# A gated DeltaNet kernel: inverses from 16-row blocks, and GpSimd's arithmetic on other engines

## The chip, the cores and the metric

The kernel runs on one core of a Trainium2 chip. The metric is the device time of one execution in microseconds, the median of several runs. The engines are PE (TensorE; PEld is its weight load), DVE (VectorE), ACT (ScalarE), POOL (GpSimd) and SP (SyncE, which here issues the DMAs). Each engine works through its own queue in order.

## The reference

A backbone of four layers over 512 tokens (256 of context, 256 noisy) of 1024 features. Layers 0 and 3 are gated DeltaNet (GDN), layer 1 is an S5 scan, layer 2 is RWKV-7; a SwiGLU FFN follows each. Of the GDN layers this matters here:

```python
def gated_delta_chunked(q, k, v, g, beta, s0):          # per head and direction
    gcum = jnp.cumsum(g, axis=-1)
    decay = jnp.where(incl, jnp.exp(jnp.where(incl, diff, 0.0)), 0.0)
    m = jnp.where(strict, jnp.einsum('bhnik,bhnjk->bhnij', k_beta, k) * decay, 0.0)
    t_inv = lax.linalg.triangular_solve(eye + m, ...)   # lower, unit diagonal
    u = jnp.einsum('bhnij,bhnjd->bhnid', t_inv, v_beta)
    w = jnp.einsum('bhnij,bhnjk->bhnik', t_inv, k_beta * jnp.exp(gcum)[..., None])
    def step(S, xs):
        v_new = u_c - jnp.einsum('bhck,bhkd->bhcd', w_c, S)
        o_c = jnp.einsum('bhck,bhkd->bhcd', q_c, S) + jnp.einsum('bhij,bhjd->bhid', a_c, v_new)
        S = S * gt[..., None, None] + jnp.einsum('bhck,bhcd->bhkd', k_c, v_new)
        return S, o_c
```

There are 8 key heads with two value heads each, and two directions. All data are float32.

## The kernel before, in words

The kernel takes chunks of 128 tokens, so a key head has 16 matrices of 128 rows to invert (4 chunks, 2 value heads, 2 directions). `Net.gdn` works head by head. While the recurrences of head g run (`GdnCore.chains`, 48 steps), other work is emitted beside them in lanes: the dense products and convolutions of coming heads (`key`, `query`, `values`, `gate`), the output of the head before (`finish`, `project`), the decay-weighted Gram matrices of head g + 2 (`gram`), the scores of head g + 1 (`scores`), and the inverses of head g + 1 (`invert`, which calls `inv128`). The chains of head g + 1 need those inverses. A scheduler then sets the order of each engine's queue from the emitted program; it may move an instruction a long way.

Three pieces are touched.

**The inverses.** `inv128` first copies the sixteen 32-row diagonal blocks of each matrix to D (`pool_copy`, L409, on POOL). `fsub` transposes them (L428) and solves 31 rows one after another: row i is a product on DVE (L439, into fsP) and a subtraction on DVE (L441, into fsT), each depending on the one before; the operands have 16 to 136 elements per partition. L444 and L471 transpose the result. After that `inv128` joins blocks of 32 to 64 and 64 to 128 rows by small matmuls (`mul`, L463) with copies from PSUM between (`evac`, which alternates ACT, L402, and DVE, L406).

**The weight split.** Every weight tile is loaded raw, rounded to its upper part on ACT (L128) and the lower part is the difference (L129, 128x512). Which engine subtracts is `self.sub`: DVE in general, POOL inside `gdn` (L537). Products use three matmuls (L135 to L137). The same `self.sub` splits activations (L159), and `norm` sets it to POOL and DVE in turn.

**Other arithmetic on POOL in `GdnCore`:** in `gram` the product of decay and Gram matrix (L1220) and its scaling per chunk (L1222, 16 per head); in `scores` the queries' decay (L1280); in `chains` the keys' decay kd (L1335, 12 per head); in `finish` a sum (L1362) and a product (L1369).

Of the kernel before, what the change touches and what calls it, by code (L numbers as in the profile page):

```python
# [19 lines left out]
P = 128  # L20
# [7 lines left out]
class Net:  # L28
# [67 lines left out]
    def banks(self, **n):  # L96
        """PSUM of a phase: banks by use, next to the two of the dense products"""
# [22 lines left out]
    def wtile(self, src):  # L120
        """-> the two parts of each block of 128 columns"""
# [84 lines left out]
    def norm(self, l, which, ts=slice(0, T), f32=None, f3=False):  # L206
# [8 lines left out]
        for k in range(KD):  # L215
# [15 lines left out]
        self.sub = nc.vector  # L231
# [86 lines left out]
    def gdn_ab(self, j, gp):  # L318
        """gates: rows of cumulated log decay (two exact parts) and per-token columns"""
# [43 lines left out]
    def conv_silu(self, ps, cw, out, segs=(0, 1)):  # L363
        """depthwise conv over each segment, then silu as h (1 + tanh h) with h half the value"""
# [19 lines left out]
    def gdn_E(self, gp, RS, ngc, m, tag, bufs, bank, eb=None):  # L384
        """E[p, f] = exp(-|gc_p - gc_f|) of one head and direction, all four chunks"""
# [25 lines left out]
    def fsub_marks(self, gp):  # L411
        """which rows (parity, unit) of a block hold the odd columns, and which the even ones"""
# [34 lines left out]

    def inv128(self, fs, A, par, W):
        """in place of one head's 16 matrices: units 0-7 the transposed inverse of 1 + L; units 8-15 the inverse, its
        rows times the token's factor"""  # L450
# [8 lines left out]
        def bank(w):  # L459
            return self.ps("i").rearrange("p (u c) -> p u c", c=w)  # L460
# [9 lines left out]
        UD = new("fsUD")  # L470
        nc.vector.transpose(UD, TD)  # L471
# [20 lines left out]
        # blocks off the diagonal of the 64-row blocks  # L492
# [34 lines left out]
    def gdn(self, l, j, last):  # L527
        nc, tc, d = self.nc, self.tc, self.d
        with self.banks(c=2, o=1, w=1, i=2), self.weights(3), \
# [5 lines left out]
            with self.open_h():  # L535
                self.norm(l, 0)
                self.sub = nc.gpsimd  # L537
# [4 lines left out]
                lanes = [Lane(core.invert(0), 41, 41),  # L542
# [8 lines left out]
                for g in range(8):  # L551
# [12 lines left out]
                    if g < 7:  # L564
                        lanes += [Lane(core.invert(g + 1), 41, 40), Lane(core.scores(g + 1), 8, 26, 16)]
# [16 lines left out]
    def s5_params(self):  # L582
        """discretisation; rows (direction, state), columns groups. A group's row of 40: powers of the diagonal by
        position (real, imaginary), input factor, diagonal, rotations exp(8 i theta 2 ** x)"""
# [8 lines left out]
        with tc.tile_pool(name="s5p", bufs=1, reuse_waits="tile") as sp:  # L593
# [37 lines left out]
            # powers of the diagonal  # L631
# [13 lines left out]
            # input factor (a - 1) / lambda  # L645
# [32 lines left out]
    def s5_prep(self, sp, pool):  # L678
        """what the mixer takes of its parameters, four groups at a time"""
# [14 lines left out]
        for i in range(16):  # L694
# [38 lines left out]
            # rotations exp(8 i theta m), m = 0 .. 63  # L733
# [18 lines left out]
            # lag kernels -7 .. 7, the skip at lag 0  # L752
# [14 lines left out]
            # block Toeplitz rows (7 - t, channel): windows of the lags  # L767
# [985 lines left out]
```

## Time and profile before

| | |
|---|---|
| runs | 4284.14 us median of 3 (4276.6 to 4288.32) |
| profiled execution | span 4284.9 us, 0.8 us above that median; it has no other time than its span |
| busy in the span | PE 87%, PEld 67%, DVE 64%, ACT 44%, POOL 32% |
| matmul instructions | 24810 |
| mean granted TensorE clock | 0.888 of full speed |
| layer 0, GDN | about 60 to 928 us of the span |
| layer 3, GDN | about 3350 to 4085 us |

In the rows, times count from the start of the span. Inside each GDN layer three stretches can be told apart: the first inverse, before any chain runs (142 to 221 and 3423 to 3501 us); six heads at their steady pace (309 to 869 and 3573 to 4029 us, each from the first chain product of one head to that of the sixth head after it); and an end without inverses. Layer 3 needs queries, gates and outputs of the second half of the tokens alone, so it has less matmul work per head. A busy engine may still run slowly, and a mean over a whole span mixes stages that have different limits.

### The profile page before, as it was taken

How to read it: one execution, taken by the hardware profiler on the slowest of the kernel's cores; microseconds unless marked ns; L12 is line 12 of the kernel's file. 1: busy time of each engine (PE TensorE's matmuls, PEld its weight loads, DVE VectorE, ACT ScalarE, POOL GpSimd, SP SyncE). 2: the span in 40 equal slices, each digit the busy share in tenths (PEclk: the TensorE clock that was granted, in tenths of full speed). 3: DMA queues.
4: the chain of work that ended last, by engine and by line, in shares of the span. 5: the costliest groups of instructions: out<-in, count | busy, mean ns of one | idle time of the engine just before them, and what ended most of it. 6: DMA issues, size and time to landing. Idle time of an engine off the chain costs nothing. (4 is left out here: it accounts for less than half of the span.)

```text
span 4284.9 us, 67673 instructions
## 1 busy us (share of the span) xinstructions
PE 3730.8 (87%) x24810; PEld 2890.9 (67%) x24810; DVE 2723.6 (64%) x5871; ACT 1865.7 (44%) x3991; POOL 1382.9 (32%) x1623
## 2 busy tenths in 40 slices
PE   4889889879999798999794999998999768888799
PEld 1566667757777686777573766665777556766698
DVE  4788878757786744333954556564333598888665
ACT  4455555553333334222543334334222455556454
POOL 1665566442222200000213434320000465666400
PEclk8889999989999899999895656678999888898899
DMA  4312111126666623443351111002444111111155
GB/s 148 111 59 78 49 45 50 43 73 191 201 203 180 239 86 123 156 157 115 129 168 57 43 31 36 28 11 91 153 158 145 60 35 43 58 52 48 45 174 161
DMA packets 243596, 432.22 MB, mean 101 GB/s; under 512 B 27968, under 2 KB 53184, under 8 KB 240832
## 3 DMA queue, kind: packets, MB, share of 16 engines
q1 hardware_dynamic: 243264, 427.90, 31.3%
q8 instruction: 195, 3.19, 0.3%
q14 instruction: 137, 1.12, 0.1%
HBM read 383.49 MB, written 44.30 MB: 100 GB/s over the span
## 5 line engine op out<-in xcount | busy, mean ns | idle before, releaser
L128 ACT CAST whi<-wraw 128x512 fp32r<-128x512 f32 (+1 forms) x906 | 553.3, 613 | 1143.4 <-PE psd L136 622.1
L129 DVE TENSOR_TENSOR wlo<-wraw,whi 128x512 fp32r<-128x512 f32 (+1 forms) x646 | 447.2, 695 | 647.8 <-ACT whi L128 633.5
L135 PE MATMUL psw<-hhi,whi 128*128 128x512 f32 (+1 forms) x1536 | 597.0, 389 | 22.3 <-ACT sz L1177 11.9
L137 PE MATMUL psw<-hhi,wlo 128*128 128x512 f32 (+1 forms) x1536 | 579.2, 377 | 0.0
L136 PE MATMUL psw<-hlo,whi 128*128 128x512 f32 (+1 forms) x1536 | 579.0, 377 | 0.1
L129 POOL TENSOR_TENSOR wlo<-wraw,whi 128x512 fp32r<-128x512 f32 x260 | 352.1, 1357 | 195.4 <-ACT whi L128 181.4
L135 PEld LDWEIGHTS psw<-hhi,whi 128*128 128x128 f32 x1536 | 304.0, 198 | 93.6 <-ACT sz L1177 13.1
L137 PEld LDWEIGHTS psw<-hhi,wlo 128*128 128x128 f32 x1536 | 300.8, 196 | 53.0 <-issue 2.1
L136 PEld LDWEIGHTS psw<-hlo,whi 128*128 128x128 f32 x1536 | 302.7, 197 | 48.5 <-issue 2.9
L135 PE MATMUL psd<-hhi,whi 128*128 128x512 f32 (+1 forms) x784 | 296.6, 378 | 16.1 <-ACT hhi L158 16.1
L441 DVE TENSOR_TENSOR fsT<-fsT,fsP 128x126 f32<-128x126 f32 (+22 forms) x744 | 287.9, 387 | 13.5
L136 PE MATMUL psd<-hlo,whi 128*128 128x512 f32 (+1 forms) x784 | 291.7, 372 | 3.8 <-DVE hlo L159 3.4
L137 PE MATMUL psd<-hhi,wlo 128*128 128x512 f32 (+1 forms) x784 | 289.9, 370 | 0.4 <-DVE wlo L129 0.4
L439 DVE TENSOR_TENSOR fsP<-fsL,fsT 128x126 f32<-128x126 f32 (+22 forms) x744 | 279.4, 376 | 14.0
L135 PE MATMUL psd<-fh,whi 128*128 128x512 f32 (+1 forms) x704 | 261.3, 371 | 0.0
L136 PE MATMUL psd<-fl,whi 128*128 128x512 f32 (+1 forms) x704 | 257.3, 366 | 0.0
L137 PE MATMUL psd<-fh,wlo 128*128 128x512 f32 (+1 forms) x704 | 256.8, 365 | 0.0
L239 DVE SCALAR_TENSOR_TENSOR X<-psd,modT,X 128x256 f32<-128x256 f32 x376 | 166.1, 477 | 128.1 <-PE psd L137 127.1
L171 PE MATMUL psm<-mraw,cs 128*32 128x256 f32 x1280 | 141.2, 412 | 63.3 <-DMA mraw<-in_modw 62.2
L135 PEld LDWEIGHTS psd<-hhi,whi 128*128 128x128 f32 x784 | 149.9, 191 | 63.4 <-ACT hhi L158 21.6
L136 PEld LDWEIGHTS psd<-hlo,whi 128*128 128x128 f32 x784 | 149.6, 191 | 35.4 <-DVE hlo L159 5.2
L137 PEld LDWEIGHTS psd<-hhi,wlo 128*128 128x128 f32 x784 | 149.7, 191 | 25.5 <-DVE wlo L129 0.8
(509 smaller groups left out, 8493.7 us busy)
## 6 DMA issues: line engine op xcount, KB each, us to landing
mraw<-in_modw SPq DMA_DIRECT2D x384, 256.0 KB, 3.4
wraw<-in_ffnin SPq DMA_DIRECT2D x352, 256.0 KB, 2.9
wraw<-in_gdn_qkvz SPq DMA_DIRECT2D x192, 256.0 KB, 2.7
wraw<-in_ffnout SPq DMA_DIRECT2D x160, 256.0 KB, 2.8
wraw<-in_gdn_out SPq DMA_DIRECT2D x64, 256.0 KB, 2.7
wraw<-in_rwkv_rkv SPq DMA_DIRECT2D x48, 256.0 KB, 3.0
s5ca<-ca SPq DMA_DIRECT2D x32, 256.0 KB, 3.3
s5in<-it SPq DMA_DIRECT2D x32, 256.0 KB, 4.2
```

The source lines that it names most:

```text
L128: nc.scalar.copy(hi[:, :n], raw[:, :n])
L129: self.sub.tensor_tensor(lo[:, :n], raw[:, :n], hi[:, :n].bitcast(F32), op=ALU.subtract)
L135: mm(out, whi, ahi, start=start, stop=False)
L136: mm(out, whi, alo, start=False, stop=False)
L137: mm(out, wlo, ahi, start=False, stop=stop)
L171: nc.tensor.matmul(ps[64 * x + 32 * q:64 * x + 32 * q + 32, :256], self.cs[:, k, :], w[:, q * 256:q * 256 + 256], start=(k == 0), stop=(k ...
L239: nc.vector.scalar_tensor_tensor(self.X[:, f, c], ps[:, c], self.modT[l][:, gate, f, s:s + 1], self.X[:, f, c], op0=ALU.mult, op1=ALU.add)
L439: nc.vector.tensor_tensor(pv, L[:, i + 1:, i:i + 1].to_broadcast([P, n, m]), X[:, i:i + 1, 0:m].to_broadcast([P, n, m]), op=ALU.mult)
L441: nc.vector.tensor_tensor(X[:, i + 1:, 0:m], X[:, i + 1:, 0:m], pv, op=ALU.subtract)
```

## The change

`sub16` takes the place of `fsub` in the GDN layers (the RWKV layer keeps `fsub`). It takes the two 16-row diagonal blocks of each 32-row block, solves both at once in 14 steps of two DVE operations with at most 56 elements, and joins them to 32 rows by two rounds of 64 small matmuls, with DVE transposes and one PSUM read between. `inv128` is then as before, with 29 emitted steps instead of 41. POOL's arithmetic in the GDN layers goes to DVE (weight splits, activation splits, L1220 and L1222 as one fused operation, L1280, L1362, L1369) and to ACT (the copies to D, kd). `norm` no longer alternates.

```diff
 def norm(...):
-                self.sub = (nc.gpsimd, nc.vector)[k % 2]
                 self.split(h[:, ts], self.hhi[k][:, ts], self.hlo[k][:, ts])
+    def sub16(self, fs, mk, D, block, bank, new):
+        even, low, odd, eye, top = mk
+        L = fs.tile([P, 1024], F32, name=self.nm("fsL"), tag="fsL")
+        A, X = [L[:, x:x + 256].rearrange("p (r c) -> p r c", c=16) for x in (512, 768)]
+        L = L[:, :512].rearrange("p (r i) -> p r i", i=32)
+        nc.vector.transpose(L, D.rearrange("p u (h r) -> p r h u", h=2))
+        nc.vector.scalar_tensor_tensor(A, L[:, :, 0:16], even, L[:, :, 16:32], op0=ALU.mult, op1=ALU.add)
+        nc.vector.tensor_tensor(X, eye, A, op=ALU.subtract)
+        for i in range(1, 15):
+            n, m = 15 - i, i
+            pv = pr[:, :n * m].rearrange("p (r c) -> p r c", c=m)
+            nc.vector.tensor_tensor(pv, A[:, i + 1:, i:i + 1].to_broadcast([P, n, m]),
+                                    X[:, i:i + 1, 0:m].to_broadcast([P, n, m]), op=ALU.mult)
+            nc.vector.tensor_tensor(X[:, i + 1:, 0:m], X[:, i + 1:, 0:m], pv, op=ALU.subtract)
+            yield
+        nc.scalar.activation(E[:, :, 0:16], xt, AF.Copy, scale=even)
+        nc.scalar.activation(E[:, :, 16:32], xt, AF.Copy, scale=low)
+        nc.vector.transpose(TD.rearrange("p u (h c) -> p c h u", h=2), E)
+        nc.vector.transpose(UD, TD)
+        pv = bank(16)
+        for u in range(16):
+            for b in range(4):
+                mm(pv[q[b], u], block(q[b], u), TD[q[b], u, 0:16], start=True, stop=True)
+        nc.vector.scalar_tensor_tensor(R, pv, odd, top..., op0=ALU.mult, op1=ALU.add)
+        pv = bank(16)
+        for u in range(16):
+            for b in range(4):
+                mm(pv[q[b], u], UD[q[b], u], R[q[b], u], start=True, stop=True)
+        self.evac(TD[:, :, 0:16], pv)
+        nc.vector.transpose(UD, TD)
 def inv128(...):
-            self.pool_copy(D[x], Z[x, :, x])
+            nc.scalar.copy(D[x], Z[x, :, x])
-        TD = yield from self.fsub(fs, par, D, new)
-        nc.vector.transpose(UD, TD)
+        TD, UD = yield from self.sub16(fs, par, D, lambda x, u: Z[x, u, x], bank, new)
 def gdn(...):
-                self.sub = nc.gpsimd
-                        lanes += [Lane(core.invert(g + 1), 41, 40), ...]
+                        lanes += [Lane(core.invert(g + 1), 29, 40), ...]
 class GdnCore: gram
-            nc.gpsimd.tensor_tensor(e, e, g, op=ALU.mult)
-                nc.gpsimd.tensor_scalar(M[...], e[:, c * P:c * P + P], be[:, hd, c:c + 1], 0.0, ...)
+                nc.vector.scalar_tensor_tensor(M[...], e[:, cs], be[:, hd, c:c + 1], g[:, cs],
+                                               op0=ALU.mult, op1=ALU.mult)
 scores
-            nc.gpsimd.tensor_tensor(eb[:, tq], eb[:, tq], q[:, tq], op=ALU.mult)
+            nc.vector.tensor_tensor(eb[:, tq], eb[:, tq], q[:, tq], op=ALU.mult)
 chains
-                    nc.gpsimd.tensor_scalar(kd, kt[:, cs], ec[hd][:, c:c + 1], 0.0, ...)
+                    nc.scalar.activation(kd, kt[:, cs], AF.Copy, scale=ec[hd][:, c:c + 1])
 finish
-        nc.gpsimd.tensor_tensor(v2(sq), v2(sq), q2, op=ALU.add)
+        nc.vector.tensor_tensor(v2(sq), v2(sq), q2, op=ALU.add)
-        nc.gpsimd.tensor_tensor(z, z, v2(r), op=ALU.mult)
+        nc.vector.tensor_tensor(z, z, v2(r), op=ALU.mult)
```

How the queues change is read from the built programs (the line numbers of the changed kernel are its own). First, GpSimd's queue in layer 3 at the steady pace, about a sixth of one head, before:

```order
L129 TENSOR_TENSOR wlo_31625<-wraw_31623,whi_31624 128x512
L129 TENSOR_TENSOR wlo_31631<-wraw_31629,whi_31630 128x512
L1335 TENSOR_SCALAR kd_31478<-kt_30718,el_30936 128x128
L1220 TENSOR_TENSOR E_31601<-E_31601,acc 128x512
L1335 TENSOR_SCALAR kd_31551<-kt_30718,el_30971 128x128
L129 TENSOR_TENSOR wlo_31723<-wraw_31721,whi_31722 128x512
L1220 TENSOR_TENSOR E_31676<-E_31676,acc 128x512
```

In the changed kernel, all of its queue for one head there (sk, a power of four numbers, and three memsets stood there before as well):

```order
L1270 TENSOR_TENSOR sk_32450<-ss_32447,half_6062_30263 128x4
L543 MEMSET M_31515 32x8x32
L544 MEMSET M_31515 32x8x32
L578 MEMSET M_31515 64x8x64
```

Nothing that reads a whole tile is left on GpSimd in a GDN layer.

Second, VectorE's queue in layer 3 while a head's rows are solved, before (x and S are the chain's two DVE steps, X the residual):

```order
L439 TENSOR_TENSOR fsP_31226<-fsL_31206,fsT_31208 128x120
L1316 SCALAR_TENSOR_TENSOR x_31423<-psc_29471,neg_29664,V_30755 128x128
L239 SCALAR_TENSOR_TENSOR X<-psd_31635,modT_84,X 128x256
L441 TENSOR_TENSOR fsT_31208<-fsT_31208,fsP_31226 128x20x6
L439 TENSOR_TENSOR fsP_31226<-fsL_31206,fsT_31208 128x133
```

and in the changed kernel near the end of the 14 steps (L481 and L483 are the new pair, L1378 is x, L1403 is S):

```order
L129 TENSOR_TENSOR wlo_32425<-wraw_32423,whi_32424 128x512
L481 TENSOR_TENSOR fsP_32256<-fsL_32224 128x26
L1403 SCALAR_TENSOR_TENSOR S_32402<-S_32213,gt_31801,psc_30265 128x128
L380 SCALAR_TENSOR_TENSOR kT_32196<-t_32278,kT_32196 128x512
L1378 SCALAR_TENSOR_TENSOR x_32415<-psc_30266,neg_30478,V_31647 128x128
L374 SCALAR_TENSOR_TENSOR q_32197<-t_32341,cw_30297,q_32197 128x255
L129 TENSOR_TENSOR wlo_32513<-wraw_32511,whi_32512 128x512
L483 TENSOR_TENSOR fsL_32224<-fsL_32224,fsP_32256 128x2x13
```

The weight splits now stand in the queue of the chain's x and S.

Third, TensorE's queue in layer 3, where the first round of the new small matmuls of that head stands (L497, 64 in all):

```order
L497 MATMUL psi_32634<-fsTD_32606,M_31515 32x16 x12
L1398 MATMUL psc_30265<-w_32509,kd_32540 128x128
L135 MATMUL psd_32569<-Y_32201,whi_32518 128x256
L136 MATMUL psd_32569<-Y_32201,whi_32518 128x256
L137 MATMUL psd_32569<-Y_32201,wlo_32519 128x256
L135 MATMUL psd_32569<-Y_32201,whi_32518 128x256
L136 MATMUL psd_32569<-Y_32201,whi_32518 128x256
L137 MATMUL psd_32569<-Y_32201,wlo_32519 128x256
L1376 MATMUL psc_30266<-S_32353,kT_30599 128x128
L497 MATMUL psi_32634<-fsTD_32606,M_31515 32x16 x31
```

The scheduler splits the rounds into pieces among the large products: 74 pieces for the 16 rounds of layer 0, 41 for those of layer 3.

## Rows read from the trace of the kernel before

**Rows 1.** Stretches of layer 0: length, then busy us of each engine.

```profile
core 0: us, PE busy (x) PEld busy (x) DVE busy (x) ACT busy (x) POOL busy (x), PEclk, DMA share, GB/s
142.00:221.00 79.00, 63.43 (x477) 42.38 (x477) 64.13 (x133) 35.98 (x86) 45.70 (x50) 0.85 0.33 107
309.00:869.00 560.00, 497.41 (x3556) 388.16 (x3555) 449.63 (x965) 309.04 (x677) 327.75 (x364) 0.95 0.17 54
869.00:928.00 59.00, 45.69 (x214) 35.62 (x215) 19.42 (x48) 26.89 (x44) 22.39 (x27) 0.86 0.06 18
```

**Rows 2.** The same of layer 3.

```profile
3423.00:3501.00 78.00, 53.69 (x440) 44.35 (x438) 71.00 (x142) 40.32 (x100) 49.51 (x55) 0.81 0.17 55
3573.00:4029.00 456.00, 374.39 (x3241) 318.37 (x3242) 398.82 (x897) 262.06 (x619) 279.66 (x340) 0.91 0.16 52
```

**Rows 3.** Groups by line, 309 to 869 us: count, busy, mean ns, idle before.

```profile
L129 POOL TENSOR_TENSOR wlo<-wraw,whi 128x512 fp32r<-128x512 f32 x91 | 122.7, 1350 | 71.5 <-ACT whi L128 66.8 <-PE psw L137 2.9 <-PE psw L136 1.3
L441 DVE TENSOR_TENSOR fsT<-fsT,fsP 128x126 f32<-128x126 f32 (+22 forms) x177 | 76.1, 430 | 3.4
L439 DVE TENSOR_TENSOR fsP<-fsL,fsT 128x126 f32<-128x126 f32 (+22 forms) x176 | 71.2, 404 | 3.6
L239 DVE SCALAR_TENSOR_TENSOR X<-psd,modT,X 128x256 f32<-128x256 f32 x96 | 41.9, 476 | 27.1 <-PE psd L137 26.6
L376 DVE SCALAR_TENSOR_TENSOR t<-t,cw,t 128x508 f32<-128x508 f32 (+1 forms) x48 | 41.8, 871 | 4.4 <-ACT t L372 3.9
L1316 DVE SCALAR_TENSOR_TENSOR x<-psc,neg,V 128x128 f32<-128x128 f32 x73 | 25.0, 346 | 22.5 <-PE psc L1314 21.9
```

**Rows 4.** Groups by line, 3573 to 4029 us.

```profile
L129 POOL TENSOR_TENSOR wlo<-wraw,whi 128x512 fp32r<-128x512 f32 x88 | 117.7, 1342 | 37.1 <-ACT whi L128 31.9 <-DVE t L376 4.0 <-DVE X L239 0.6
L441 DVE TENSOR_TENSOR fsT<-fsT,fsP 128x126 f32<-128x126 f32 (+22 forms) x176 | 78.7, 447 | 2.5
L439 DVE TENSOR_TENSOR fsP<-fsL,fsT 128x126 f32<-128x126 f32 (+22 forms) x176 | 78.0, 443 | 2.8
```

**Rows 5.** Longest waits of PE, 3573 to 4029 us: total us, times, longest.

```profile
PE psc L1319 <- DVE x L1316: 15.6, 11, 4.3
PE psi L1199 <- DVE kT L382: 13.2, 4, 4.4
```

**Rows 6.** DVE in order of time: start us, us, line.

```profile
3576.10 0.30 DVE L439 TENSOR_TENSOR fsP<-fsL,fsT 128x133 f32<-128x133 f32 x1
...
3578.37 1.25 DVE L441 TENSOR_TENSOR fsT<-fsT,fsP 128x126 f32<-128x126 f32 x1
```

**Rows 7.** POOL at the same time.

```profile
3577.82 0.37 POOL L1335 TENSOR_SCALAR kd<-kt,el 128x128 f32<-128x128 f32 x1 [3.60 <-PE psc L1336]
3578.16 1.31 POOL L129 TENSOR_TENSOR wlo<-wraw,whi 128x512 fp32r<-128x512 f32 x1
```

**Rows 8.** DVE in order of time, operations of three sizes.

```profile
3560.39 0.68 DVE L1203 TENSOR_TENSOR acc<-psi,SU 128x512 f32<-128x512 f32 x1
3560.98 0.21 DVE L441 TENSOR_TENSOR fsT<-fsT,fsP 128x56 f32<-128x56 f32 x1
3561.11 0.42 DVE L382 SCALAR_TENSOR_TENSOR sz<-t,sz 128x256 f32<-128x256 f32 x1
```

**Rows 9.** DVE in order of time, the last row of a block and a transpose.

```profile
196.43 0.17 DVE L439 TENSOR_TENSOR fsP<-fsL,fsT 128x16 f32<-128x16 f32 x1
196.85 1.17 DVE L444 STREAM_TRANSPOSE fsTD<-fsT 128x512 f32<-128x512 f32 x1
```

**Rows 10.** PE in order of time: large products and pieces of small ones.

```profile
267.32 1.20 PE L463 MATMUL psi<-fsTD,M 32*32 32x32 f32 x64 [0.66 <-DVE fsTD L444]
...
538.53 0.38 PE L1331 MATMUL pso<-E,w 128*128 128x128 f32 x2
538.75 0.39 PE L1336 MATMUL psc<-w,kd 128*128 128x128 f32 x2
539.07 0.43 PE L463 MATMUL psi<-fsTD,M 32*32 32x32 f32 x14
```

More of the change, by code (lines that the diff above doesn't have):

```diff
@@ L446, in fsub, with sub16_consts @@
         return TD
+    def sub16_consts(self, gp):
+        nc = self.nc
+        even, low = self.fsub_marks(gp)
+        odd = gp.tile([P, 1], F32, name=self.nm("par"), tag="par2")
+        nc.vector.tensor_scalar(odd, low, -1.0, None, op0=ALU.mult)
+        eye = gp.tile([P, 16, 16], F32, name=self.nm("eye16"), tag="eye16")
+        nc.gpsimd.memset(eye, 0.0)
+        nc.gpsimd.memset(eye.rearrange("p r c -> p (r c)")[:, ::17], 1.0)
+        top = gp.tile([P, 16], F32, name=self.nm("top16"), tag="top16")
+        nc.gpsimd.memset(top, 0.0)
+        for b in range(4):
+            nc.gpsimd.affine_select(out=top, in_=top, compare_op=ALU.not_equal, fill=1.0, base=-32 * b,
+                                    pattern=[[-1, 16]], channel_multiplier=1)
+        return even, low, odd, eye, top
@@ new lines, in sub16 @@
+    def sub16(self, fs, mk, D, block, bank, new):
+        nc = self.nc
+        mm = nc.tensor.matmul
+        even, low, odd, eye, top = mk
+        q = [slice(32 * b, 32 * b + 32) for b in range(4)]
+        L = fs.tile([P, 1024], F32, name=self.nm("fsL"), tag="fsL")
[5 more added lines that the diff above has]
+        yield
+        pr = fs.tile([P, 64], F32, name=self.nm("fsP"), tag="fsP")
+        for i in range(1, 15):
[4 more added lines that the diff above has]
+            nc.vector.tensor_tensor(X[:, i + 1:, 0:m], X[:, i + 1:, 0:m], pv, op=ALU.subtract)
+            yield
+        E = new("fsE")
+        xt = X.rearrange("p r c -> p c r")
+        nc.scalar.activation(E[:, :, 0:16], xt, AF.Copy, scale=even)
+        nc.scalar.activation(E[:, :, 16:32], xt, AF.Copy, scale=low)
+        TD = new("fsTD")
+        nc.vector.transpose(TD.rearrange("p u (h c) -> p c h u", h=2), E)
+        yield
+        UD = new("fsUD")
+        nc.vector.transpose(UD, TD)
[3 more added lines that the diff above has]
+                mm(pv[q[b], u], block(q[b], u), TD[q[b], u, 0:16], start=True, stop=True)
+        yield
+        R = A
+        nc.vector.scalar_tensor_tensor(R, pv, odd, top.unsqueeze(1).to_broadcast([P, 16, 16]), op0=ALU.mult,
+                                       op1=ALU.add)
+        pv = bank(16)
+        for u in range(16):
+            for b in range(4):
+                mm(pv[q[b], u], UD[q[b], u], R[q[b], u], start=True, stop=True)
+        yield
+        self.evac(TD[:, :, 0:16], pv)
+        UD = new("fsUT")
+        nc.vector.transpose(UD, TD)
+        yield
+        return TD, UD
@@ L459, in bank @@
         def bank(w):
-            return self.ps("i").rearrange("p (u c) -> p u c", c=w)
+            return self.ps("i")[:, :min(T, 16 * w)].rearrange("p (u c) -> p u c", c=w)
         def mul(o, x, y):
@@ L541, in gdn @@
                     pass
-                lanes = [Lane(core.invert(0), 41, 41),
+                lanes = [Lane(core.invert(0), 29, 41),
                          Lane(chain(core.query(0), core.values(0), core.key(1)), 22, 30),
@@ L1151, in __init__ @@
         self.bank = [net.ps("c") for _ in range(2)]
-        self.par = net.fsub_marks(gp)
+        self.par = net.sub16_consts(gp)
         self.W = self.new("W", 1, [P, 8, 64])
@@ L1219, in gram @@
             e = net.gdn_E(self.gp, self.RS, self.ngc, m, "Em", 2, "i")
-            nc.gpsimd.tensor_tensor(e, e, g, op=ALU.mult)
             for c in range(4):
-                nc.gpsimd.tensor_scalar(M[:, (hd % 2) * 8 + (hd // 2) * 4 + c], e[:, c * P:c * P + P],
-                                        be[:, hd, c:c + 1], 0.0, op0=ALU.mult, op1=ALU.add)
+                cs = slice(c * P, c * P + P)
+                nc.vector.scalar_tensor_tensor(M[:, (hd % 2) * 8 + (hd // 2) * 4 + c], e[:, cs], be[:, hd, c:c + 1],
+                                               g[:, cs], op0=ALU.mult, op1=ALU.mult)
             yield
```

5 lines of the change are left out of this document (1 added, 4 removed).

## The prediction

> **What bounds the kernel now.** I read first the busy times by stretch, then the groups by line in the steady stretches, then the waits, and last a few moments in order of time.
>
> The change acts in layers 0 and 3 alone, so the shares of the whole span say little. In the six steady heads of layer 0 a head takes 560 / 6 = 93.3 us; PE is busy 89% of that, DVE 80%, POOL 59%, ACT 55% [rows 1]. In layer 3 a head takes 456 / 6 = 76.0 us, with PE at 82% and DVE at 87% [rows 2]. The longest waits of PE there are for DVE [rows 5]: layer 3 is bound by DVE's queue. In layer 0 both queues press: DVE itself stood idle 49 us for PE at two lines, the residual and the chain's x [rows 3]. In the first inverse of each layer DVE is busy 81% and 91% [rows 1, 2].
>
> Next, how DVE spends that time. The two lines of the substitution take 147 us of its 450 in layer 0 and 157 of its 399 in layer 3, at means of 404 to 447 ns [rows 3, 4]. Yet one operation with 133 elements takes 0.30 us while POOL waits for the chain; 2 us later one with 126 elements takes 1.25 us, and is over 0.15 us after a POOL operation of 1.31 us that began just before it [rows 6, 7]. So a DVE operation that meets one of POOL's long ones waits that one out, and a good part of DVE's busy time is such waiting. This is the reading on which the forecast stands.
>
> **The change, part by part.** All prices are DVE time for one head at the steady pace, layer 0 / layer 3.
>
> *POOL falls silent.* Clean prices of the substitution are 0.17 us at 16 elements, 0.21 at 56 and 0.30 at 133 [rows 6, 8, 9]; its operations have 92 elements in the mean, which makes 0.25. The excess of the two lines is (147 - 353 x 0.25) / 6 = 9.8, and (157 - 352 x 0.25) / 6 = 11.5. Others suffer as well: the convolution's line stands at 871 ns [rows 3] against 0.68 for 512 elements [rows 8], 0.19 on each of 8 a head, 1.5 us, and I allow the same on some 15 more of that length. Taken: -14 / -15. The ends are -10, if those two lines alone are disturbed, and -17.
>
> *Fewer and smaller steps.* 62 operations at 0.25 become 28 of 14 to 56 elements at 0.20, between the prices for 16 and 56: -15.5 + 5.6 = -9.9. Added are one transpose more than before (1.17 [rows 9]), three passes of 256 elements (0.42 each [rows 8]), half of a PSUM copy of at most that size. Net -7.4. It can't be a loss: 28 at the old 0.25 still leaves -6. The prices at 16 and 133 elements differ by less than a factor of two, so much of each is a fixed cost of the instruction. The Trainium skill ("VectorE: DVE Perf Modes", section on the TRN2 errata) says that operations from SBUF pay a fixed latency per instruction, and advises tiles of 512 elements and more, which speaks against a step of 14 elements; if the whole price were fixed, this term would be -6 and no more.
>
> *What moves onto DVE.* From one start to the next, 512 elements cost 0.59 us where the next operation doesn't depend on them [rows 8]; 256 elements 0.42 - 0.09 = 0.33; 128 elements with a factor per row 0.346 [rows 3] less that overlap, 0.26. A head has 15.2 / 14.7 weight splits (91 and 88 for six heads [rows 3, 4]): 8.9 / 8.7. The fused Gram scaling, 16 at 0.26: 4.2. The queries' decay, 4: 2.4 / 1.3. Sum, product and split of the output, three for each segment, two segments in layer 0 and one in layer 3: 3.5 / 1.8. Together +19.0 / +16.0.
>
> *DVE's sum* is -14 - 7.4 + 19.0 = -2.4 in layer 0, -15 - 7.4 + 16.0 = -6.4 in layer 3. At today's shares of 80% and 87% the head becomes shorter by 3.0 and 7.3 us. Seven heads each have an inverse beside them: -21 and -51.
>
> *The first inverses.* Nothing but a few dense products runs beside them, and DVE's share is the same or higher. One head's relief of -14 - 7.4 stands against some 10 weight splits, one Gram and one set of decays, about +12; over those shares this is -11 and -12.
>
> *The ends.* Six output operations a layer lie one after another there; a POOL operation of 512 elements takes 1.35 us [rows 3] and DVE's 0.68 [rows 8]. With the last splits I take -5 a layer, between 0 and -10.
>
> *What PE gets.* A round of 32-row products, 64 instructions, took 1.20 us [rows 10]; each new round is of that kind with twice the instructions over twice the row groups, and I take the same, up to 2.4. A piece set among large products costs a little more: 0.32 us passed from the start of the product before it to its own, where 0.22 passed between two large ones [rows 10], so 0.1 a piece. Layer 0: 16 x 1.2 + 74 x 0.1 = 27 us, or 3.3 a head; layer 3: 23 us, or 2.9. PE is idle 10 us a head in layer 0 and 14 in layer 3 [rows 1, 2], so I cost this at nothing; where that cover is gone it costs all of it, and that is a rival below. The Trainium skill ("TensorEngine Tiling (Array Packing)", section Key Properties) says that a change of the tiling mode drains TensorE, which speaks against small products strewn among large ones. The row shows a switch at 0.1 us; a full drain would show the tail of the large product, 0.39 - 0.22 = 0.17 (an estimate from the same rows), some 8 us more over all 115 pieces.
>
> *ACT* gets at most 12 kd, 4 copies and 3 more a head, none above 512 elements; at 0.7 us, more than DVE takes for 512 [rows 8], that is 13 us, and it is idle 42 us a head [rows 1]. Cost nothing. On POOL kd waited 3.6 us for the chain once [rows 7]; on ACT this holds up the eviction queued behind it, which needs the same chain a step later. In the norms POOL's half of the splits goes to DVE: one of four, a microsecond either way.
>
> Sum: -21 - 51 - 23 - 10 = -105. The profiled execution's span is 4284.9 us, 0.8 above the median of the runs: **4180 us**. With the ends of the first term (4 us of DVE a head one way, 2 to 3 the other), of the second and of the layers' ends the forecast's own range is 4130 to 4230.
>
> **The rivals.**
>
> *Tighter packing* (20%). With POOL's random delays gone, the queues may pack better than now. If DVE reached 90% in both loops, a head would take 72.5 / 0.9 = 80.6 and 60.1 / 0.9 = 66.8 us: -89 and -64, with -33 for first inverses and ends. **4099 us.** For it: PE waits for DVE rather than the other way in layer 3 [rows 5]. Against it: in layer 0 PE is 89% busy already.
>
> *PE decides in layer 0* (18%). Then what DVE saves there is worth nothing and the 27 us of small products come on top, while layer 3 gains 51 + 12 + 5: 4285 + 27 - 68 = **4244 us**. For it: DVE's waits for PE [rows 3]. Against it: PE's granted clock is at 0.95 there, so it has idled at times too [rows 1].
>
> *DVE's queue waits for weights* (12%). On POOL a weight split waited for the rounding on ACT: 66.8 us over 91 of them, 31.9 over 88 [rows 3, 4], 0.55 in the mean. POOL had little queued behind; DVE has the chain's x and S. If each of the 239 splits (15.2 and 14.7 for 8 heads each) holds DVE as long, that is +131: **4311 us**, slower. It decides from 105 / 239 = 0.44 us a split. Against it: the scheduler may set a split later in a queue that has other work.
>
> *The long DVE operations aren't POOL's doing* (2%). Then the first term is nothing, DVE's sum is +11.6 / +8.6, and over the same shares and seven heads the loops lose 101 and 69: about **4455 us**. The pair in [rows 6, 7] speaks against it. That nothing changes, because the scheduler hides both sides, I give 1%.
>
> **How the numbers follow.** The forecast has 47%. About 13 us, or 0.3%, is what a measurement of this kernel tells from no change. Forecast, tighter packing and PE's bound all lie beyond that: 85% faster. Of the 12% of waiting splits, 3 fall within it at a mean wait near 0.44 us; with the 1% of no change, 4% same. The other 9 and the 2% make 11% slower. The range of 4090 to 4265 leaves out the waiting splits' larger part and the better half of tighter packing, some 2 in 10.
>
> **What would show it.** Right: POOL busy under 5 us in a steady stretch; DVE's two solving lines at means of 0.17 to 0.25 us; weight splits on DVE at 0.68 to 0.70 and idle before them under 0.2 us each; six heads in some 540 us in layer 0 and 412 in layer 3; the first inverses some 11 us shorter. Wrong: DVE's idle before weight splits above 0.44 us each; PE's busy share in layer 0 above 95% with an unchanged head; solving steps that still take over a microsecond; or DVE waiting for the two rounds of small products.

## The result, and the profile after

The changed kernel takes 4119.9 us, the median of four runs (4110.9 to 4127.8); the kernel before takes 4286.2 us in the same comparison. The ratio is 0.961, with a 95% interval of 0.958 to 0.963. The forecast of 4180 us had the direction right and missed the size by 60 us; the time lies inside the range of 4090 to 4265. Two executions of a later kernel, at 10843 and 5841 us, were heavily disturbed (TensorE was far slower in all layers), and their times are not used.

The busy times of the changed kernel by stretch answer to [rows 1, 2]: the first inverse, the first head, and six heads, of layer 0 and then of layer 3 (columns as there).

```profile
137.00:214.00 77.00, 67.35 (x769) 45.26 (x767) 54.92 (x134) 44.28 (x106) 2.14 (x4) 0.93 0.35 117
219.00:276.00 57.00, 49.78 (x697) 39.86 (x696) 46.12 (x129) 43.46 (x102) 1.13 (x3) 0.92 0.06 20
276.00:827.00 551.00, 517.33 (x5180) 405.84 (x5179) 423.89 (x1033) 363.97 (x805) 14.16 (x28) 0.97 0.18 60
3335.00:3406.00 71.00, 57.67 (x709) 46.92 (x707) 56.12 (x145) 48.12 (x116) 2.67 (x4) 0.88 0.19 61
3412.00:3458.00 46.00, 40.48 (x597) 33.95 (x595) 32.09 (x109) 30.99 (x79) 1.13 (x3) 0.66 0.01 2
3458.00:3868.00 410.00, 378.35 (x4899) 324.52 (x4900) 356.37 (x955) 317.97 (x764) 11.81 (x23) 0.98 0.19 63
```

The first head (from its first chain product to the next head's) stood in no row of before; there it was:

```profile
226.00:309.00 83.00, 67.42 (x509) 51.61 (x509) 70.98 (x155) 46.04 (x101) 47.98 (x57) 0.84 0.14 46
3505.00:3573.00 68.00, 53.12 (x461) 44.50 (x459) 60.04 (x152) 39.96 (x99) 42.07 (x61) 0.79 0.09 28
```

POOL is all but silent (14 and 12 us in six heads, memsets and a small power). A steady head takes 91.8 us in layer 0 (93.3 before) and 68.3 in layer 3 (76.0); PE is now busy 94% and 92% of it. The first heads lost 26 and 22 us. In layer 0 this division misleads: work slides past the mark between two heads, and the second head grew by the same marks from 80 us (309 to 389) to 111 (276 to 387), while the five after it fell from 480 to 440 together. The seven heads as a whole, before and after in layer 0, then before and after in layer 3, are the safer measure:

```profile
226.00:869.00 643.00, 564.84 (x4062) 439.77 (x4062) 520.61 (x1119) 355.08 (x777) 375.73 (x420) 0.93 0.17 53
219.00:827.00 608.00, 567.12 (x5875) 445.70 (x5874) 470.01 (x1161) 407.44 (x906) 15.29 (x31) 0.97 0.17 57
3505.00:4029.00 524.00, 427.51 (x3702) 362.87 (x3701) 458.86 (x1048) 302.01 (x718) 321.73 (x400) 0.89 0.15 49
3412.00:3868.00 456.00, 418.83 (x5496) 358.48 (x5495) 388.45 (x1063) 348.97 (x841) 12.93 (x26) 0.95 0.18 57
```

They got 35 and 68 us shorter. PE's idle time, length less busy time, fell from 78 to 41 and from 96 to 37 us; its busy time hardly changed although the small products came on top, since the same products ran at a higher granted clock.

DVE's groups in layer 3, which answer to [rows 4] (in layer 0 the means are the same within 2 ns, and the weight splits waited 26.3 us over 94):

```profile
L129 DVE TENSOR_TENSOR wlo<-wraw,whi 128x512 fp32r<-128x512 f32 x96 | 65.9, 686 | 6.5 <-ACT whi L128 5.8 <-ACT w L1386 0.2
L374 DVE SCALAR_TENSOR_TENSOR t<-t,cw,t 128x508 f32<-128x508 f32 (+1 forms) x48 | 35.8, 746 | 2.8 <-ACT t L370 2.1
L1378 DVE SCALAR_TENSOR_TENSOR x<-psc,neg,V 128x128 f32<-128x128 f32 x73 | 25.0, 343 | 2.2 <-PE psc L1376 1.5
L1284 DVE SCALAR_TENSOR_TENSOR M<-E,be,acc 128x128 f32<-128x128 f32 x80 | 22.4, 348 | 0.4 <-ACT E L393 0.3
L483 DVE TENSOR_TENSOR fsL<-fsL,fsP 128x50 f32<-128x50 f32 (+6 forms) x75 | 14.8, 198 | 1.0
```

The solving lines went from 0.44 us to 0.20, the convolution from 0.871 [rows 3] to 0.746, while x, which reads the chain's product in PSUM, stayed at 0.34. The longest waits of PE in layer 3, after [rows 5]:

```profile
PE psw L135 <- ACT q L370: 6.4, 6, 2.4
PE psc L1381 <- DVE x L1378: 6.0, 11, 1.0
```

Added up over all rows of that view, PE's waits for DVE in the six heads of layer 3 fell from 73 us to 10, and in layer 0 from 47 to 17. Those for ACT rose in layer 3 from 8 to 21.

Where the 165 us between the two profiled executions went, and what each later kernel did to the same stages (layer 0 from the first scaling in its norm to that in the next norm; RWKV and layer 3 from the last product of the FFN before them to the next norm's splits; the last three columns are the six heads of layer 3, PE's waits added up as above):

| kernel | median us | layer 0 | RWKV | layer 3 | six heads | DVE busy | PE waits for DVE |
|---|---|---|---|---|---|---|---|
| before | 4286 | 867 | 915 | 728 | 456 | 399 | 73 |
| after | 4120 | 818 | 890 | 643 | 410 | 356 | 10 |
| before again | 4290 | 872 | 924 | 732 | | | |
| old substitution, POOL silent | 4192 | 835 | 898 | 701 | 452 | 392 | 30 |
| 16-row blocks, POOL as before | 4251 | 863 | 921 | 709 | 448 | 341 | 35 |
| idle additions on POOL | 4472 | 945 | 921 | 838 | 531 | 493 | 84 |
| weight splits on POOL | 4206 | 836 | 898 | 701 | 462 | 363 | 39 |
| kd and copies on POOL | 4144 | 809 | 918 | 648 | 415 | 362 | 16 |
| rounds made twice | 4248 | 856 | 908 | 705 | 448 | 347 | 8 |
| weight splits made twice | 4222 | 831 | 922 | 699 | 450 | 411 | 25 |
| RWKV without POOL | 4124 | 820 | 904 | 640 | | | |

The GDN layers gave 49 + 85 = 134 us. RWKV, which the change does not touch, gave 25, S5 some 6. RWKV's time goes up and down by as much in the kernels below, so their GDN layers say more than their medians.

### The profile page after: what moved, and what is told of

Read it like the earlier page. It is cut to its first block, busy times and chain, and to the rows that moved or that the text cites. A ratio compares the mean times of both kernels' runs of the same rounds, so it can differ in the third digit from the quotient of the medians.

```text
span 4120.3 us, 75194 instructions
## 1 busy us (share of the span) xinstructions
PE 3692.1 (90%) x28906; PEld 2865.7 (70%) x28906; DVE 2596.9 (63%) x6045; ACT 1984.0 (48%) x4291; POOL 486.7 (12%) x625
## 4 chain that ended last, share of the span: by engine, by line
PE 73%; DVE 12%; ACT 8%; DMA 3%; issue 2%; POOL 1%; SPq 0%; DVEq 0%; ACTq 0%; POOLq 0%
PE psd L135 10%; PE psd L136 10%; PE psd L137 9%; PE psw L135 7%; PE psw L136 7%; PE psw L137 7%; DMA mraw<-in_modw 2%; PE psm L171 2%; PE psg L1527 2%; PE psi L528 2%; PE pso L1670 1%; PE pso L1668 1%; PE psc L1381 1%; PE pso L1393 1%; DVE wlo L129 1%
## 5 line engine op out<-in xcount | busy, mean ns | idle before, releaser
L129 DVE TENSOR_TENSOR wlo<-wraw,whi 128x512 fp32r<-128x512 f32 (+1 forms) x906 | 622.6, 689 | 711.3 <-ACT whi L128 684.1
L135 PEld LDWEIGHTS psd<-fh,whi 128*128 128x128 f32 x704 | 132.9, 189 | 34.5 <-ACT whi L128 11.1
L137 PEld LDWEIGHTS psd<-fh,wlo 128*128 128x128 f32 x704 | 133.0, 189 | 21.7
L136 PEld LDWEIGHTS psd<-fl,whi 128*128 128x128 f32 x704 | 133.0, 189 | 21.6 <-issue 1.6
```

Source lines behind the costliest of these rows:

```text
L129: self.sub.tensor_tensor(lo[:, :n], raw[:, :n], hi[:, :n].bitcast(F32), op=ALU.subtract)
L135: mm(out, whi, ahi, start=start, stop=False)
L136: mm(out, whi, alo, start=False, stop=False)
L137: mm(out, wlo, ahi, start=False, stop=stop)
```

## The experiments

**The two halves of the change, each alone.** First the old substitution, with POOL silent:

```diff
-        TD, UD = yield from self.sub16(fs, par, D, lambda x, u: Z[x, u, x], bank, new)
+        TD = yield from self.fsub(fs, par, D, new)
+        UD = new("fsUD")
+        nc.vector.transpose(UD, TD)
...
```

> The changed kernel with the old substitution of 31 rows put back; GpSimd's arithmetic stays on VectorE and ScalarE. Contention (the prediction's reading: a VectorE operation waits out GpSimd's long ones): with GpSimd silent the two solving lines have means of 0.24 to 0.27 us although they are the old ones, and VectorE has 7 to 9 us more per head than in the changed kernel; a steady head of layer 3 takes 75 to 78 us, one of layer 0, where TensorE is 94% busy, 92 to 96; in all 4190 to 4240 us. Rival (the steps alone give the gain, the long operations are VectorE's own): the solving lines stay at 0.38 us or more, VectorE gets 16 to 19 us per head on top of what it had before, and the whole takes 4400 us or more.

It took 4192 us (ratio to before 0.978, 0.975 to 0.981). DVE's solving lines, layer 3:

```profile
L439 DVE TENSOR_TENSOR fsT<-fsT,fsP 128x126 f32<-128x126 f32 (+22 forms) x180 | 45.5, 253 | 1.7
L437 DVE TENSOR_TENSOR fsP<-fsL,fsT 128x126 f32<-128x126 f32 (+22 forms) x180 | 45.4, 252 | 1.6
```

The same instructions that took 0.445 us [rows 4] take 0.25 when POOL is silent, the very clean price that the prediction had worked out. The rival of 4400 us and more is out: the long operations were POOL's doing. The six heads of layer 3 came to 75.3 us each, as expected. In layer 0 six heads came to 85.5 each, less than the expected 92 to 96, and the seven heads to

```profile
229.00:838.00 609.00, 555.11 (x4072) 440.54 (x4072) 514.67 (x1376) 400.75 (x886) 18.98 (x37) 0.91 0.17 56
```

which is the 608 us of the changed kernel: there the silence, with the moves that make it, gives the heads all that the whole change gives them, with DVE at 515 us instead of 470.

Then the other half: 16-row blocks, with all of POOL's arithmetic back.

```diff
-            nc.scalar.copy(D[x], Z[x, :, x])
+            self.pool_copy(D[x], Z[x, :, x])
...
+                self.sub = nc.gpsimd
...
```

> The changed kernel with all of GpSimd's arithmetic in the GDN layers back on GpSimd as before (weight splits, Gram scaling, decays, output sums, copies to D); only the substitution by 16-row blocks is kept. Contention: its 28 operations have means of 0.32 to 0.40 us, since GpSimd is busy again, but VectorE is rid of 16 to 19 us a head of other work, so its time per head in layer 3 falls to 54 to 57 us; if VectorE's sum decides, a head of layer 3 takes 62 to 66 us, below the 68.3 of the changed kernel, and the whole 4070 to 4110 us: the moves off GpSimd would have been a loss beside the smaller steps. Rival (what matters of the moves is not VectorE's sum but that weights, kd and copies come 0.7 to 1.4 us earlier in their chains): a head of layer 3 takes over 70 us and TensorE waits for GpSimd, in all 4150 to 4230 us.

4251 us (0.990, 0.987 to 0.994). The six heads of layer 3, by stretch:

```profile
3565.00:4013.00 448.00, 395.93 (x4823) 335.83 (x4822) 341.19 (x724) 274.35 (x649) 291.14 (x346) 0.92 0.18 57
```

and DVE's groups by line there:

```profile
L483 DVE TENSOR_TENSOR fsL<-fsL,fsP 128x54 f32<-128x54 f32 (+6 forms) x76 | 26.5, 349 | 1.4
L1379 DVE SCALAR_TENSOR_TENSOR x<-psc,neg,V 128x128 f32<-128x128 f32 x73 | 25.0, 344 | 19.3 <-PE psc L1377 18.8
L481 DVE TENSOR_TENSOR fsP<-fsL 128x54 f32<-128x54 f32 (+6 forms) x76 | 24.2, 318 | 1.6
```

DVE's sum did what the arithmetic said, 56.9 us a head; the time did not follow. With DVE busy 76% a head takes 74.7 us, where the changed kernel, with more work on DVE, takes 68.3. So the expectation that goes by the sum fell. What moved with the time is PE's waiting for DVE, 35 us here and 10 there, and its granted clock, 0.92 here and 0.98 there. No wait of PE there names POOL itself, so the rival as stated is not shown either (4251 us is beyond its 4230, and RWKV has 31 of the 131 us over the changed kernel).

The halves do not add up. In the two GDN layers the first gives 32 + 27 = 59 us over before and the second 4 + 19 = 23; together they give 134. Each is worth more beside the other, above all in layer 3.

**Contention by itself.** Nothing but idle work is added on POOL:

```diff
+                for _ in range(4):
+                    nc.gpsimd.tensor_tensor(self.idle, self.idle, self.idle, op=ALU.add)
...
```

> The changed kernel, and beside each weight tile of a GDN layer four additions of 128x352 zeros on GpSimd, which nothing reads: some 60 a head, so that GpSimd is as busy as before the change and nothing waits for it. Contention: the means of the two solving lines rise from 0.196 us to 0.30 to 0.42, the convolution's from 0.745 to 0.85 or more, VectorE gets 7 to 12 us more a head, a head of layer 3 takes 74 to 80 us, and the whole 4170 to 4240 us. Rival (the long operations are VectorE's own, or come from waits on GpSimd's results): all means stay within 0.02 us and the time within 13 us of the changed kernel's 4120.

4472 us (1.042, 1.039 to 1.046), 352 us more than without the idle work, and far more than either theory gave. The GDN layers have 127 + 195 = 322 of it; RWKV, where nothing was added, has 31. The six heads of layer 3, by stretch:

```profile
3689.00:4220.00 531.00, 428.19 (x4891) 363.69 (x4891) 493.32 (x956) 320.26 (x760) 318.23 (x361) 0.85 0.15 49
```

and DVE's groups by line there:

```profile
L130 DVE TENSOR_TENSOR wlo<-wraw,whi 128x512 fp32r<-128x512 f32 x96 | 76.0, 791 | 4.0 <-ACT whi L129 3.5
L1291 DVE SCALAR_TENSOR_TENSOR M<-E,be,acc 128x128 f32<-128x128 f32 x80 | 58.3, 790 | 0.0
L487 DVE TENSOR_TENSOR fsL<-fsL,fsP 128x50 f32<-128x50 f32 (+6 forms) x75 | 44.0, 586 | 1.0
L1385 DVE SCALAR_TENSOR_TENSOR x<-psc,neg,V 128x128 f32<-128x128 f32 x73 | 24.8, 339 | 2.1 <-PE psc L1383 1.6
L241 DVE SCALAR_TENSOR_TENSOR X<-psd,modT,X 128x256 f32<-128x256 f32 x48 | 22.5, 473 | 2.4 <-PE psd L141 2.3
L477 DVE STREAM_TRANSPOSE fsL<-fsD 128x512 f32<-128x512 f32 x5 | 5.4, 1072 | 0.0
```

POOL is busy 318 us in six heads, DVE gets 137 us more for the same operations, and which of them grow is plain: a solving step goes from 0.198 to 0.586 us, the Gram scaling from 0.348 to 0.790, by 0.39 and 0.44 us, where an addition is on POOL for 0.91 in the mean; x and the residual, which have one tile in PSUM, and the transposes (1.07 us both times), which have one input, do not grow at all. Sorted by whether an addition was running when DVE's operation began, the same trace gives the two solving lines 0.70 and 0.72 us with one and 0.18 without, and the weight split 1.07 (27 of 96) and 0.68. The Trainium skill ("SBUF — State Buffer", section "Who interferes with whom") says that a VectorE instruction with two SBUF inputs contends with a GpSimd instruction that reads SBUF, and that one with at most one such input, outside the modes that use both ports, does not; these rows agree.

The same with scalings of one input in place of the additions:

> As the run with idle additions on GpSimd (4472 us), but each is a scaling of one input instead of an addition of two. If what counts is that GpSimd reads SBUF at all: the solving lines have means of 0.40 us or more again, and the time is 4400 us or more so long as the operations are as long; x, which reads PSUM, stays at 0.34 us. If it is GpSimd's second input that meets VectorE's: the lines stay at 0.20 to 0.25 and the time within 30 us of 4120.

> The run with idle scalings of one input on GpSimd again, since its first profile was of a disturbed execution. Its other time was 4231 us. If what counts is that GpSimd reads SBUF at all: the solving lines have means of 0.27 to 0.45 us, the fused Gram scaling (both its tiles in SBUF) 0.45 or more, x and the residual (one tile in PSUM) 0.34 and 0.48 as ever; 4200 to 4260 us, less than with two inputs because one operation is 0.55 us instead of 0.92. If it takes GpSimd's second input: the solving lines stay at 0.20.

Of each, one run can be used, 4231 and 4237 us, where the second expectation had 4200 to 4260. The profiles are of the executions of 10843 and 5841 us. DVE's durations can still be read in them; in layer 3 of the second:

```profile
L1291 DVE SCALAR_TENSOR_TENSOR M<-E,be,acc 128x128 f32<-128x128 f32 x80 | 30.8, 449 | 0.0
L1385 DVE SCALAR_TENSOR_TENSOR x<-psc,neg,V 128x128 f32<-128x128 f32 x73 | 25.0, 342 | 18.8 <-PE psc L1383 17.7
L485 DVE TENSOR_TENSOR fsP<-fsL 128x50 f32<-128x50 f32 (+6 forms) x75 | 19.1, 255 | 0.8
```

One input on POOL is enough to lengthen the solving steps (0.198 to 0.255) and the Gram scaling (0.348 to 0.449), though the solving steps by less than either expectation named; POOL was busy 24% of that stretch. How the harm grows with POOL's load for this form stays open.

**Which of the moves counted.** The weight splits, with the splits of the outputs, alone back on POOL (one line, `self.sub = nc.gpsimd` after the norm):

> The changed kernel with the weight splits (and the splits of the outputs) of the GDN layers back on GpSimd; all else as changed. Some 15 operations of 1.36 us a head, that is GpSimd busy about a quarter of the time. Theory of single waits (after the runs with the old substitution, with GpSimd's arithmetic back and with idle additions: what TensorE waits for is a single late x or S, and a VectorE operation is late when it meets one of GpSimd's that reads SBUF; VectorE's sum is not what decides): the two solving lines rise from 0.196 us to 0.24 to 0.32, TensorE's waits for VectorE in the steady heads grow from 17 and 10 us to 20 to 40 each, and the kernel takes 4140 to 4200 us though VectorE has less to do. Rival (VectorE's sum decides): VectorE is rid of 10 us a head and gets 4 to 6 back in longer operations, so a head of layer 3 takes 62 to 66 us and the kernel 4070 to 4105.

4206 us (0.980, 0.978 to 0.982), a little beyond the first theory's 4200. POOL's 128 us of splits (1.34 us each) raise the solving lines to 0.29 us, and DVE, rid of 66 us of splits, is at 363 us against 356 in the six heads of layer 3: the relief is eaten whole by longer operations. By stretch, layer 3:

```profile
3491.00:3953.00 462.00, 403.80 (x4900) 345.67 (x4901) 363.43 (x856) 315.84 (x764) 147.79 (x125) 0.93 0.17 56
```

and the longest of PE's waits there, which is for the chain's S:

```profile
PE psc L1377 <- DVE S L1404: 12.4, 4, 4.1
```

At nearly the same sum on DVE a head takes 77.0 us instead of 68.3. No wait of PE there names a split on POOL, so it is not that the weights came later; of the 52 us over the changed kernel, 27 are PE's waits and 25 the same products at a granted clock of 0.93 instead of 0.98.

kd and the copies to D alone back on POOL:

> The changed kernel with the keys' decay kd (12 a head) and the copies to D (4 a head) back on GpSimd instead of ScalarE: some 10 us of GpSimd a head in operations of one input, and 6 to 8 us less on ScalarE, for which TensorE waits 15 and 21 us in the two steady stretches now. Theory of single waits: GpSimd's operations read SBUF and lengthen VectorE's as any other does, and kd takes 0.57 to 0.67 us instead of 0.41 in the chain; the kernel takes 4130 to 4170 us. Rival (short operations of one input do no harm, ScalarE's relief counts): 4085 to 4110 us.

4144 us (0.965, 0.963 to 0.968), within the first theory, but not for its reason. The two GDN layers take 809 + 648 us, as much as in the changed kernel (818 + 643); the 24 us are RWKV's, which took 918. These short operations may stand on either engine.

**Is DVE's sum the bound?** Each weight split made twice on DVE:

```diff
-            self.sub.tensor_tensor(lo[:, :n], raw[:, :n], hi[:, :n].bitcast(F32), op=ALU.subtract)
+            for _ in range(1 + self.twice):
+                self.sub.tensor_tensor(lo[:, :n], raw[:, :n], hi[:, :n].bitcast(F32), op=ALU.subtract)
...
```

> The changed kernel with each weight split of the GDN layers made twice on VectorE (the second with the same result): 15 operations of 0.69 us, 10.4 us more VectorE work a head and no work on GpSimd. If VectorE's sum sets the head, as the prediction reckoned (sum over the share of 77% or 87%): a head gets 12 to 13 us longer, 15 heads in all, and the kernel takes 4290 to 4320 us. If TensorE decides and VectorE's work counts only where a single operation that TensorE waits for comes late: the heads get 2 to 6 us longer, and the kernel takes 4150 to 4210 us, although VectorE is then as busy as with idle additions on GpSimd (86% and 93%, 4472 us).

4222 us (0.985, 0.983 to 0.986), between the two expectations; RWKV has 32 of the 102 us over the changed kernel. The seven heads of layer 0, then the six of layer 0 and of layer 3:

```profile
221.00:836.00 615.00, 569.27 (x5862) 445.53 (x5860) 524.90 (x1260) 407.80 (x903) 17.17 (x31) 0.96 0.17 56
291.00:836.00 545.00, 506.63 (x5096) 397.06 (x5096) 462.45 (x1097) 354.23 (x782) 14.58 (x27) 0.96 0.18 58
3515.00:3965.00 450.00, 396.09 (x4899) 336.96 (x4899) 410.50 (x1046) 318.35 (x765) 11.98 (x23) 0.94 0.18 58
```

In layer 0 a head of the seven gets 1.0 us longer (615 against 608) for 7.8 more of DVE's; the six alone even look shorter (545 against 551), by the marks. In layer 3 a head gets 6.7 us longer for 9.0 more of DVE's. So DVE's sum counts in layer 3, at 87% and more, and hardly in the heads of layer 0, at 77%.

**The price of the small products.** Both rounds of 64 made twice:

```diff
+        for _ in range(2):
             for u in range(16):
                 for b in range(4):
                     mm(pv[q[b], u], block(q[b], u), TD[q[b], u, 0:16], start=True, stop=True)
...
```

> The changed kernel with each of the two rounds of 64 small products made twice (the second time with the same result): 4.4 us more TensorE work a head by the busy times of its two lines (16.0 + 10.5 us for six heads). If the rounds are hidden, as the prediction cost them: the time stays within 13 us of 4120. If TensorE decides now (it is 94% and 92% busy in the steady heads): the heads get 3 to 5 us longer each, 15 heads in all, and the kernel takes 4150 to 4195 us.

4248 us (0.991, 0.987 to 0.994): 128 us more, beyond both expectations; in the profile 38 in layer 0, 62 in layer 3 and 18 in RWKV. The two rounds in six heads of layer 3, first in the changed kernel, then here:

```profile
L497 PE MATMUL psi<-fsTD,M 32*32 32x16 f32 x768 | 10.3, 180 | 0.2 <-ACT E L392 0.2
L505 PE MATMUL psi<-fsL,fsUD 32*32 32x16 f32 x768 | 9.7, 180 | 0.0
```

```profile
L498 PE MATMUL psi<-fsTD,M 32*32 32x16 f32 x1536 | 16.5, 184 | 11.5 <-issue 11.5
L507 PE MATMUL psi<-fsL,fsUD 32*32 32x16 f32 x1536 | 16.0, 182 | 11.1 <-issue 11.1
```

They grew from 20.2 to 55.1 us with their idle time, 5.8 a head; a head grew by 6.3. In layer 0 a head grew by 3.7 (95.5 against 91.8) for 4.1 of their busy and idle time. Nothing hides the second half of them: more work on TensorE is paid in full or nearly so in both layers. In layer 0 TensorE decides; in layer 3, where the doubled splits cost most of their time too, both queues do. The price of the first half can't be read off this, since the doubled rounds cost more than twice the single ones.

**The layer that nobody touched.** The kernel before, again:

> The kernel before, unchanged, a second time. The RWKV layer, which the change does not touch, took 915 us before and 890 after, with another order in its queues. If the order makes the difference, the layer takes 912 to 918 us again, with a granted clock of 0.65 to 0.67 in its chains (0.66 before, 0.70 after). If it is chance of the granted clock, it differs from 915 by more than 5 us.

4290 us (1.000, 0.999 to 1.002). RWKV took 924 us, 9 more than the first time, so chance of the granted clock is worth some 9 us there. But the orders of DVE's queue in RWKV fall into two families, read from ten traces as the longest sequence of rows in common in its chains: before, before again, 16-row blocks with POOL, idle additions, kd on POOL, splits twice and rounds twice share one (92% of the rows or more) and take 908 to 924 us; after, the old substitution with POOL silent and the weight splits on POOL share another (95% or more; 76 to 78% in common with the first) and take 890 to 898. The chains of RWKV (its first 297 us are alike), before and after:

```profile
2330.00:2948.00 618.00, 564.22 (x4936) 410.63 (x4936) 358.61 (x1034) 222.89 (x588) 201.71 (x281) 0.66 0.11 33
```

```profile
2273.00:2867.00 594.00, 545.64 (x4972) 395.09 (x4966) 358.81 (x1034) 222.62 (x590) 203.89 (x282) 0.70 0.11 34
```

The work is the same, the busy time of DVE too; PE runs at a higher granted clock in the second order (0.67 to 0.70 in its three traces, 0.63 to 0.66 in the seven of the first). That the order makes the clock and the time is not shown, only that they go together. Why the scheduler turns to the one or the other was not tried.

Does POOL's silence help there too? Its arithmetic in RWKV moved to DVE and ACT:

> The changed kernel, with GpSimd's arithmetic in the RWKV layer also moved, to VectorE and ScalarE; its products, its substitution of 31 rows and the GDN layers are as in the changed kernel. GpSimd is busy a third of the time in its chains now, the solving lines there have means of 0.29 us, and TensorE is 92% busy at a granted clock of 0.70. If GpSimd's operations are what makes VectorE's results late here too: the solving lines fall to 0.24 to 0.26, and the layer, 890 us now, to 850 to 880, the kernel to 4080 to 4110 us. If TensorE's own work sets the layer: 885 to 925 us, by the clock alone, and the kernel within 30 us of 4120.

4124 us (0.962, 0.960 to 0.964), as the changed kernel. The chains by stretch, and one of the solving lines in them:

```profile
2274.00:2881.00 607.00, 561.79 (x4784) 407.98 (x4784) 390.85 (x1122) 276.07 (x740) 9.38 (x18) 0.64 0.10 32
```

```profile
L439 DVE TENSOR_TENSOR fsT<-fsT,fsP 128x126 f32<-128x126 f32 (+22 forms) x217 | 54.8, 253 | 4.2
```

The solving lines fell from 0.29 to 0.25 us and the layer did not get shorter (904 us against 890). PE is busy 93% there and DVE 64%, as the second expectation has it. The test is not clean: the moves add 32 us to DVE and 53 to ACT in these chains, and the order of DVE's queue is a third one (62 to 66% in common with either family).

## Why the prediction was right, and where it was short

*What bounds the kernel.* The reading of [rows 6, 7], that a DVE operation waits out one of POOL's, is shown twice over: the old instructions at 0.25 us once POOL is silent, and the new ones at 0.59 once it is busy with work that concerns nobody. This was the step that gave the sign, and it holds.

*"POOL falls silent", -14 / -15.* This term was undersized, and it is the step that fell short. The kernel with the old substitution has the moves and the silence alone. From the first chain product of the first head to that of the eighth its DVE is busy (75.5 + 439.2) / 7 = 73.5 us a head in layer 0 and (54.3 + 391.9) / 7 = 63.7 in layer 3, against (71.0 + 449.6) / 7 = 74.4 and (60.0 + 398.8) / 7 = 65.5 before. The moves were priced at +19.0 and +16.0, so at those prices the silence was worth -20 and -18, beyond the end of -17. I had counted the solving lines, the convolution and 15 more operations; the idle additions show that others with two tiles in SBUF suffer as well, the Gram scaling and the decays among them, and that what is lost depends little on the length: 0.52 to 0.55 us for a step of 0.18 that meets an addition, 0.39 for a split of 0.68.

*Fewer and smaller steps, -7.4.* After minus that kernel, DVE is at 67.1 against 73.5 and 55.5 against 63.7: -6.4 and -8.2. The steps cost 0.197 us where 0.20 was taken. The one transpose more that the term charged with 1.17 us costs nothing in sum, for the old first one had 1024 elements and took 1.95: four take 3.6 us a head now, three took 3.8. The fixed latency per instruction that the Trainium skill names ("VectorE: DVE Perf Modes", section on the TRN2 errata) shows in them: sizes from 14 to 56 elements differ fourfold, and the times only from 0.16 to 0.22 us. The term had allowed for it.

*What moves onto DVE.* A split takes 0.686 us of busy time, as said; the fused Gram scaling 0.348.

*From DVE's sum to the head.* The sum fell by 7.2 and 10.1 us a head over the seven heads, and these got shorter by 35 us in layer 0 and 68 in layer 3, or 5.0 and 9.7 each; the forecast was 21 and 51. Divided by the shares of 80% and 87%, as I had it, those sums would have made 63 and 81 us: the rule gave too much, most of all in layer 0, and the term above too little, so that the forecast came as near as it did is partly luck. The sum is not the cause as I had it: with splits on POOL the sum is the same and a head 8.7 us longer, with all arithmetic there it is smaller and a head 6.3 us longer. In the runs with POOL's long operations PE waits for DVE 29 to 84 us in a layer's six heads (10 and 17 in the changed kernel), on single operations such as the chain's x and S. In layer 0 the smaller steps gave the heads nothing net of their small products: with 73.5 us of DVE a head (the old substitution, POOL silent) the seven take as long as with 67.1.

*First inverses and ends.* What lies before the first chain became 7 and 14 us shorter (forecast 11 and 12), but of this the first inverses themselves have only 2 and 7 (79 to 77 us, 78 to 71), where I had put all of it; the ends became 7 and 3 shorter (forecast 5 each).

*PE's small products, costed at nothing.* Their size was near: 26.5 and 20.0 us in six heads are 4.4 and 3.3 a head (forecast 3.3 and 2.9; what a switch between small and large products costs by itself was not tried). That the cover holds was wrong, as far as the doubled rounds show it: a second set is paid in full in layer 3 and nearly so in layer 0. A head became shorter nonetheless, because all of PE's waits in the six heads fell from 62 to 33 us and from 82 to 31, and the granted clock rose from 0.95 to 0.97 and from 0.91 to 0.98.

*The rivals.* Tighter packing is nearest in time (4099), but DVE's share did not rise: 77% and 87%. PE's bound came, at 94% in layer 0, after a gain and not in place of one. Waiting splits: 0.28 us of idle time each in layer 0, a little over the 0.2 that I named, and 0.07 in layer 3, far from 0.44. Of the other signs, POOL's 14 and 12 us are over the 5 that I named, and layer 0's six heads took 551 us, not 540.

*What stood in no term.* 25 of the missing 60 us are RWKV's, which go with the order of its queues; 29 are the two GDN layers' (134 against 105), the rest S5's.

## What to carry to other kernels

Before work is moved between VectorE and GpSimd, look in the trace for VectorE operations with two tiles in SBUF that take twice their usual time beside a GpSimd operation: moving GpSimd's work onto VectorE can then lower VectorE's own busy time or leave it as it was. A sum of busy times prices such a move only roughly; ask which single operations the bound engine waits for, and what that engine will decide once they come in time, since the next microsecond on it is then paid nearly in full. Try the halves of a change alone before adding them up: here they gave 59 and 23 us, and 134 together. Where work slides past the marks between heads, measure over all heads together. And compare the stages that a change doesn't touch: a scheduler may reorder them, and 25 us went with that here.

## What was not expected of the hardware

Operations on GpSimd that nothing depends on cost 322 us in the GDN layers. Among DVE's operations of one input, a copy of four elements from SBUF also grew, from 0.166 to 0.360 us, while a transpose of 512 did not. Copies of 32x256 met no addition there; with all of POOL's arithmetic back they took 0.84 us when they began beside it and 0.29 otherwise. The groups of the copy of four elements, in layer 3 of the changed kernel and then with idle additions:

```profile
L1338 DVE COPY el<-E 128x4 f32<-128x4 f32 x24 | 4.0, 166 | 2.9 <-ACT E L393 2.7
```

```profile
L1345 DVE COPY el<-E 128x4 f32<-128x4 f32 x24 | 8.7, 360 | 1.7 <-ACT E L397 1.6
```

The Trainium skill ("SBUF — State Buffer", section "Who interferes with whom") counts copies among the operations that can enter a mode with both ports; whether these ran in such a mode was not tried.

And PE's waiting is paid twice: in the six heads of layer 3 the same products keep PE busy 378 us at a granted clock of 0.98, in the changed kernel, and 428 us at 0.85 with the idle additions, where it waits 102 us instead of 31.
